# First product stage of a hybrid attention block: more buffers, and the output weights split one unit behind their load

## The chip, the cores and the metric

The kernel runs on one core of a Trainium2 chip. The metric is the device time of one execution in microseconds (us), the median over the runs of a kernel. TensorE is called PE and its weight loads PEld; VectorE is DVE, ScalarE is ACT, GpSimd is POOL, and SyncE is SP, which here issues nearly all of the DMAs. PEclk is the TensorE clock that was granted, as a share of full speed.

## The reference, cut to what matters

One layer of a streaming encoder on 2064 tokens (2048 and 16 learned ones) of width 1024. One projection W_in of 3592 columns feeds three groups of heads: a gated linear recurrence (RG-LRU), a forgetting attention and an RWKV-7 recurrence. Their outputs are joined and projected by W_out; a gated feed-forward part follows.

```python
h += rms_norm(W_out @ concat(rg_lru(p_a), forgetting_attention(p_b), rwkv7(p_c)), g_post)   # p = W_in @ rms_norm(h, g_pre)
h += rms_norm(W_down @ (gelu(g) * v), g_ffn_post)                  # [g | v] = causal_dwconv3(W_up @ rms_norm(h))
```

All is float32. The kernel keeps that precision by writing each factor as a high and a low part, hi = round(x) and lo = x - hi, and by adding three products: hi·hi, lo·hi and hi·lo (`mm3`, lines 172 to 174).

## The kernel before, in words

The program is written in a tile language. It names tiles from pools of so many buffers, and when the program is built, a scheduler with its own timing model fixes the order of the instructions on every engine, and which buffer each tile gets. On the chip each engine runs its list in that order. A tile that takes a buffer waits for the last reader of the tile that had it before, and an instruction that waits holds up all that stand behind it on its engine. `issue_after(ins)` puts the instructions of a block behind `ins` in the list of their engine.

**The first product stage** (to about 890 us) computes the projection in three parts of tokens, each of two blocks (400 and 384, 384 and 384, 256 and 256 tokens). `w_in_norm` normalises and transposes a part's rows: `norm_transpose` loads 128 rows to `xt`, an ACT Square to `xj` (L118) sums their squares, DVE scales `xt` (L130), PE transposes to `pst` (L143), and ACT and DVE write the parts `xh` and `xl` (L149, L150). `w_in_part` then does the gate columns (`fraw`, `fw`) and 24 units of 128 columns: 8 for RWKV-7 (c), 4 for the gated recurrence (a), 4 each for keys (k), values (v) and queries (q). A unit is 24 matmuls for each block into a PSUM tile `psp`. Part 0 loads raw weights and splits them into `wh` and `wl` (ACT L166, DVE L167), storing both in `scr_wk`; parts 1 and 2 load the pair from there (L216). Results of c and a leave as `stp` (L56 or L58, ACT and DVE in turns); those of k and q as `sth` and `stl` (ACT L234, DVE L235), each followed by its store; values are transposed and leave as `stv`.

**Beside the units** run the recurrences: `Beside` takes two steps of them per unit from unit 14 of a part on. They are `gate_block`, `Rwkv.block` (tiles whose names begin with `rw`, small products in `rps`, `eps`) and `lru_block` (tiles `rwlu`, `rwla`, `rwlr`; L1401 loads, L1408 is its first ACT step, and its result is stored to `scr_mix` from the buffer `lu`). They have buffers of their own. Two more jobs lie beside parts 1 and 2: `up_sums` on POOL, a step at every even unit, and `w_out_split`, a step at every odd unit of part 1: a load of 128 rows of W_out to `raw`, the ACT rounding (L166) and the DVE difference (L167) to two tiles `wo`, and two stores.

Pools: `nt` has four buffers of 4 KB a partition (tag `nt_x`: `xt`, raw weights, the three tiles of a W_out step), `w` has two each of `wh` and `wl`, and `st` two, but `stl` and `stv` one. After the stage come the attention (to about 1560 us), W_out and the feed-forward part.

Of the kernel before, what the change touches and what calls it, by code (L numbers as in the profile page):

```python
# [8 lines left out]
F32 = mybir.dt.float32  # L9
# [9 lines left out]
P = 128  # L19
D = 1024  # L20
# [12 lines left out]
class Core:  # L33


    def __init__(self, tc, ctx):
        self.tc = tc
        self.nc = tc.nc
        self.ctx = ctx
        self.uid = 0  # L40
        nc = self.nc
        self.const = ctx.enter_context(tc.tile_pool(name="const", bufs=1))
        self.ident = self.const.tile([P, P], F32, name="ident")
        make_identity(nc, self.ident[:])
        self.flip = 0
        self.root = self.apart = False

    def n(self, s):
# [3 lines left out]
    def evac(self, out, src):  # L52

        self.flip ^= 1
        if self.flip:
            self.nc.scalar.activation(out, src, AF.Copy)  # L56
        else:
            self.nc.vector.tensor_copy(out, src)  # L58
# [62 lines left out]

def norm_transpose(core, pools, psum, src, rows, gain, pieces):

    nc = core.nc
    xt = pools["nt"].tile([P, D], F32, tag="nt_x", name=core.n("xt"))
    nc.sync.dma_start(xt[:rows], src)
    junk = pools["st"].tile([P, D], BF16, tag="stv", name=core.n("xj"), bufs=1)
    v = pools["nt"].tile([P, 6], F32, tag="rs", name=core.n("rs"))
    rs = rstd_of(core, v[:rows], xt[:rows], D, junk[:rows])
    nc.vector.scalar_tensor_tensor(xt[:rows], xt[:rows], rs, gain[:rows], op0=ALU.mult, op1=ALU.mult)  # L130
    transpose_split(core, psum, xt, rows, pieces)
# [29 lines left out]
def load_parts(core, raws, src, hi, lo):  # L161

    pool, tag, bufs = raws
    raw = pool.tile(list(hi.shape), F32, tag=tag, name=core.n("raw"), bufs=bufs)
    core.loaded = core.nc.sync.dma_start(raw[:], src)
    core.nc.scalar.activation(hi, raw[:], AF.Copy)  # L166
    core.nc.vector.tensor_tensor(lo, raw[:], hi, op=ALU.subtract)  # L167
# [19 lines left out]
def w_in_norm(core, pools, psum, x, meta, gain, part):  # L187
    blocks = []
    for b, tl in enumerate(w_in_tokens(part)):
        t0 = tl[0][0]  # L190
        n = sum(r for _, r in tl)
        hi = pools["xn"].tile([P, KD, n], F32R, tag=f"xh{b}", name=core.n("xh"))
        lo = pools["xn"].tile([P, KD, n], F32R, tag=f"xl{b}", name=core.n("xl"))
        blocks.append((t0, n, tl, hi, lo))
    for t0, n, tl, hi, lo in blocks:
        for s, rows in tl:
            src = meta if s < META else x[s - META : s - META + rows, :]
            norm_transpose(core, pools, psum, src, rows, gain, [(hi, lo, s - t0, 0, rows)])
    return blocks
# [7 lines left out]
def w_in_weights(core, pools, w_in, c0, scr, part):  # L207

    if part == 0:
        src = w_in[:, c0 : c0 + P].rearrange("(k p) c -> p k c", p=P)  # L210
        pair = split_load(core, pools["w"], (pools["nt"], "nt_x", None), src, [P, KD, P], "w")
    else:
        pair = [pools["w"].tile([P, KD, P], F32R, tag=s, name=core.n(s)) for s in ("wh", "wl")]
    for t, kept in zip(pair, w_in_kept(scr, c0)):
        t = t[:].rearrange("p k c -> p (k c)").bitcast(F32)
        core.loaded = core.nc.sync.dma_start(*((kept, t) if part == 0 else (t, kept)))  # L216
    return pair


def w_in_step(core, pools, psum, weights, block, kind, c0, scr):  # L220
# [8 lines left out]
    if kind in ("q", "k"):  # L229
        sc = 0.125 if kind == "q" else 1.0  # L230
        r0 = c0 - (512 if kind == "q" else 1024)
        oh = st.tile([P, 400], F32R, tag="sth", name=core.n("sth"))
        ol = st.tile([P, 400], F32R, tag="stl", name=core.n("stl"), bufs=1)
        nc.scalar.activation(oh[:, :n], ps[:, :n], AF.Copy, scale=sc)  # L234
        nc.vector.scalar_tensor_tensor(ol[:, :n], ps[:, :n], sc, oh[:, :n], op0=ALU.mult, op1=ALU.subtract)  # L235
        nc.sync.dma_start(scr[kind + "h"][r0 : r0 + P, t0 : t0 + n], oh[:, :n].bitcast(F32))
        nc.sync.dma_start(scr[kind + "l"][r0 : r0 + P, t0 : t0 + n], ol[:, :n].bitcast(F32))
        return
# [7 lines left out]
    def turn():  # L246
# [3 lines left out]
        for i, (s, rows) in enumerate(tl):  # L250
            nc.tensor.transpose(pt[:rows, i], o[:, s - t0 : s - t0 + rows], core.ident[:])
        ot = st.tile([P, 4, P], F32, tag="stv", name=core.n("stv"), bufs=1)
        i0 = 0
# [15 lines left out]
def w_in_gate(core, pools, psum, w_in, blocks, scr, part):  # L269
# [5 lines left out]
    if part == 0:  # L275
        raw = pools["w"].tile([P, KD, 8], F32, tag="fraw", name=core.n("fraw"), bufs=1)
        nc.sync.dma_start(raw[:], w_in[:, c0 : c0 + 8].rearrange("(k p) c -> p k c", p=P))
# [6 lines left out]
    for t0, n, tl, hi, lo in blocks:  # L284
# [5 lines left out]
        nc.scalar.activation(a[:, :n], ps[32:40, :n], AF.Copy)  # L290
        o = pools["st"].tile([8, 400], F32, tag="stl", name=core.n("fo"), bufs=1)
        nc.vector.tensor_tensor(o[:, :n], ps[0:8, :n], a[:, :n], op=ALU.add)
# [585 lines left out]
def rwkv_consts(core, pool, psum, w):  # L878
# [70 lines left out]

    k["st"] = c.tile([P, 2, 64], F32, name="rstate")  # L950
    nc.vector.memset(k["st"][:], 0.0)


    u1 = c.tile([P, 256], F32, name="unit1")
    nc.vector.memset(u1[:], 0.0)
    nc.vector.memset(u1[:, 0:256:17], 1.0)
    u2 = c.tile([P, 128], F32, name="unit2")
    nc.vector.memset(u2[:], 0.0)
    nc.vector.memset(u2[0:64, 0:128:17], 1.0)
    nc.vector.memset(u2[64:128, 8:128:17], 1.0)  # L960
    k["unit"] = {1: u1, 2: u2}
    return k


class Rwkv:
# [127 lines left out]
    def chunks(self, b, nch, sg, rav, bk, wc, bon):  # L1093
# [54 lines left out]
        x3 = ix[:np_, : 16 * jw].rearrange("p (j s) -> p j s", s=16)  # L1148
        nc.vector.tensor_copy(ix[:np_, : 16 * jw], k["unit"][parts][:np_, :])
        nc.vector.memset(ia[:np_, 0:256:17], 1.0)  # L1150
# [96 lines left out]

        st = self.t([P, nch + 1, 2, 64], "st")
        nc.vector.tensor_copy(st[:, 0], k["st"][:])
        gain = self.ps().rearrange("p (c a t) -> p c a t", a=2, t=64)  # L1250
# [8 lines left out]
        for c in range(nch):  # L1259
# [7 lines left out]
            nc.vector.tensor_copy(st[:, c + 1], gain[:, c])  # L1267
        nc.vector.tensor_copy(k["st"][:], st[:, nch])
        yield
# [117 lines left out]
def lru_block(core, R, scr, k, b):  # L1387
# [8 lines left out]
    def tl(s):  # L1396
        return R.t([P, 256], s)[:, :n]

# [67 lines left out]
def w_out_split(core, pool, w_out, scr):  # L1466

    for k in range(KD):
        hi, lo = (pool.tile([P, D], F32R, tag="nt_x", name=core.n("wo")) for _ in range(2))
        load_parts(core, (pool, "nt_x", None), w_out[k * P : (k + 1) * P, :], hi[:], lo[:])  # L1470
        for i, t in enumerate((hi, lo)):
            core.nc.sync.dma_start(scr["wo"][k, i], t[:].bitcast(F32))
        yield
# [585 lines left out]
def hybrid_block_kernel(ctx: ExitStack, tc: tile.TileContext, args, out):  # L2059
# [25 lines left out]
    with ExitStack() as p1:  # L2085
# [7 lines left out]
        with ExitStack() as p1a:  # L2093
# [6 lines left out]
            for part in range(3):  # L2100
# [29 lines left out]
                for i, _ in enumerate(units, READY + 1 if part == 0 else 1):  # L2130
                    if i == READY + 1:
                        beside.add(recurrences(core, R, lk, a["fox_f_bias"], scr, blocks, part))
                    beside.advance()
                    if part and (i % 2 == 0 or part == 1 and i > 1):
                        with tc.issue_after(core.loaded.ins):
                            next(split_out if i % 2 else sums, None)
                run(sums) if part == 2 else None
# [182 lines left out]
```

## Time and profile before

| | before |
|---|---|
| median of 3 runs | 3050.18 us (3047.77 to 3064.09) |
| the profiled execution, its time | 3044.26 us |
| its span in the trace | 3042.5 us |
| granted PE clock over the span | 0.977 |
| busy: PE, PEld, DVE, ACT, POOL | 95%, 82%, 67%, 49%, 43% |
| DMA, mean over the span | 174 GB/s |

A busy share is the time in which an engine worked, over the span. Matmuls are pipelined, so a busy PE need not be PE at its peak: the weight loads run under the matmuls, and at a lower granted clock the same matmul is counted as busy for longer. In the views of the trace, a row of waits names the engine and its instruction, what released it, and the total, the number and the longest of those waits.

### The profile page before, as it was taken

How to read it: one execution, taken by the hardware profiler on the slowest of the kernel's cores; microseconds unless marked ns; L12 is line 12 of the kernel's file. 1: busy time of each engine (PE TensorE's matmuls, PEld its weight loads, DVE VectorE, ACT ScalarE, POOL GpSimd, SP SyncE). 2: the span in 40 equal slices, each digit the busy share in tenths (PEclk: the TensorE clock that was granted, in tenths of full speed). 3: DMA queues.
4: the chain of work that ended last, by engine and by line, in shares of the span. 5: the costliest groups of instructions: out<-in, count | busy, mean ns of one | idle time of the engine just before them, and what ended most of it. 6: DMA issues, size and time to landing. Idle time of an engine off the chain costs nothing. (4 is left out here: it accounts for less than half of the span.)

```text
span 3042.5 us, 52754 instructions
## 1 busy us (share of the span) xinstructions
PE 2901.8 (95%) x18694; PEld 2486.7 (82%) x18694; DVE 2043.7 (67%) x3947; ACT 1480.9 (49%) x2858; POOL 1309.2 (43%) x1567
## 2 busy tenths in 40 slices
PE   6998999999989998999989899999999999999998
PEld 6998898888876654565568899999999999787887
DVE  5268645656677885555736888888778777646666
ACT  4245342434346654454634656666666665434333
POOL 1001121122224656566843457545655544556443
PEclk9998999999998999999999999999999999999999
DMA  6776478565654347434326555567677764536453
GB/s 211 245 233 214 155 237 294 159 212 193 213 160 95 97 102 214 110 94 123 82 81 221 166 168 181 180 187 221 210 220 208 216 204 130 167 109 213 146 182 120
DMA packets 469189, 530.48 MB, mean 174 GB/s; under 512 B 85710, under 2 KB 355736, under 8 KB 467372
## 3 DMA queue, kind: packets, MB, share of 16 engines
q1 hardware_dynamic: 468156, 526.17, 56.6%
q8 instruction: 147, 2.41, 0.3%
q0 software_dynamic: 768, 0.93, 0.1%
q14 instruction: 118, 0.97, 0.1%
HBM read 368.07 MB, written 158.90 MB: 173 GB/s over the span
## 5 line engine op out<-in xcount | busy, mean ns | idle before, releaser
L172 PE MATMUL psu<-xo,uw 128*128 128x344 f32 x1848 | 591.3, 324 | 15.6 <-DVE vb L1812 7.9
L173 PE MATMUL psu<-xo,uw 128*128 128x344 f32 x1848 | 593.9, 322 | 0.0
L174 PE MATMUL psu<-xo,uw 128*128 128x344 f32 x1848 | 585.0, 321 | 0.7 <-DVE uw L1621 0.7
L172 PE MATMUL psp<-xh,wh 128*128 128x384 f32 (+2 forms) x1152 | 382.9, 332 | 4.2 <-ACT wh L166 3.1
L174 PE MATMUL psp<-xh,wl 128*128 128x384 f32 (+2 forms) x1152 | 380.3, 331 | 2.0 <-DMA wl<-scr_wk 1.8
L173 PE MATMUL psp<-xl,wh 128*128 128x384 f32 (+2 forms) x1152 | 379.5, 330 | 0.0
L172 PEld LDWEIGHTS psu<-xo,uw 128*128 128x128 f32 x1848 | 348.1, 189 | 19.1 <-DVE vb L1812 9.9
L1621 DVE TENSOR_TENSOR uw<-uq,uw 128x512 fp32r<-128x512 f32 x341 | 316.9, 936 | 67.9 <-ACT uw L1620 65.8
L173 PEld LDWEIGHTS psu<-xo,uw 128*128 128x128 f32 x1848 | 349.2, 189 | 0.0
L174 PEld LDWEIGHTS psu<-xo,uw 128*128 128x128 f32 x1848 | 347.7, 189 | 1.3 <-DVE uw L1621 1.2
L1620 ACT ACTIVATE uw<-uq 128x512 fp32r<-128x512 f32 x462 | 287.0, 627 | 105.0 <-PE psu L174 47.8
L686 ACT ACTIVATE p<-sc,bias 128x512 f32<-128x512 f32 (+4 forms) x352 | 197.4, 590 | 191.3 <-PE sc L682 159.1
L559 DVE TENSOR_REDUCE mc<-mx 128x1 f32<-128x512 f32 (+6 forms) x352 | 190.3, 564 | 105.2 <-PE mx L554 79.9
L1760 DVE SCALAR_TENSOR_TENSOR uy<-psu,ffn_cols,uy 128x342 f32<-128x342 f32 (+1 forms) x390 | 220.2, 566 | 57.4 <-ACT uy L1758 55.7
L1768 POOL TENSOR_TENSOR uy<-uy,uy 128x342 f32<-128x342 f32 (+1 forms) x132 | 139.3, 1056 | 249.8 <-DVE uy L1760 63.7
L1621 POOL TENSOR_TENSOR uw<-uq,uw 128x512 fp32r<-128x512 f32 x121 | 180.9, 1495 | 148.4 <-ACT uw L1620 130.5
L725 POOL TENSOR_TENSOR acc<-acc,p 128x512 f32<-128x512 f32 (+3 forms) x208 | 221.2, 1066 | 52.3 <-DVE acc L725 26.3
L174 PEld LDWEIGHTS psp<-xh,wl 128*128 128x128 f32 x1152 | 221.3, 192 | 11.5 <-issue 6.0
L172 PEld LDWEIGHTS psp<-xh,wh 128*128 128x128 f32 x1152 | 221.4, 192 | 11.0 <-issue 4.0
L173 PEld LDWEIGHTS psp<-xl,wh 128*128 128x128 f32 x1152 | 221.2, 192 | 7.7 <-issue 5.6
L1621 DVE TENSOR_TENSOR fo<-u,fo 128x896 fp32r<-128x896 f32 x88 | 100.1, 1138 | 132.7 <-ACT fo L1620 132.2
L1620 ACT ACTIVATE fo<-u 128x896 fp32r<-128x896 f32 x88 | 81.2, 923 | 207.1 <-PE psd L174 115.6
(483 smaller groups left out, 6399.2 us busy)
## 6 DMA issues: line engine op xcount, KB each, us to landing
uq<-scr_us SPq DMA_DIRECT2D x220, 256.0 KB
uq<-in_ffn_up_dram SPq DMA_DIRECT2D x209, 256.0 KB
wl<-scr_wk SPq DMA_DIRECT2D x48, 512.0 KB
wh<-scr_wk SPq DMA_DIRECT2D x48, 512.0 KB
u<-scr_ff SPq DMA_DIRECT2D x88, 256.0 KB
scr_ff<-uy SPq DMA_DIRECT2D x110, 171.0 KB
raw<-in_w_in_dram SPq DMA_DIRECT2D x24, 512.0 KB
scr_wk<-wh SPq DMA_DIRECT2D x24, 512.0 KB
```

What stands on the lines that cost most here:

```text
L172: nc.tensor.matmul(out, ah, bh, start=first, stop=False, skip_group_check=more)
L173: nc.tensor.matmul(out, ah, bl, start=False, stop=False, skip_group_check=more)
L174: nc.tensor.matmul(out, al, bh, start=False, stop=last, skip_group_check=more)
L559: self.reduced = nc.vector.tensor_reduce(mc[:rows, i, ci : ci + 1], ps[:rows, : e - a], axis=AX.X, op=ALU.max)
L686: last = nc.scalar.activation(p[:rows, :w], ps[:rows, :w], AF.Exp, bias=bias[:rows, j : j + 1])
L725: eng.tensor_tensor(a, ps_[0][0][:rows, c0:n] if start and i == 1 else a, p[:rows, : n - c0], op=ALU.add)
L1620: core.nc.scalar.activation(hi, src, AF.Copy)
L1621: (eng or core.nc.vector).tensor_tensor(lo, src, hi, op=ALU.subtract)
L1760: core.conved = stt(y[:, :n], src[:, i : n + i], cw[:, 44 * i + cc : 44 * i + cc + 1], y[:, :n], op0=ALU.mult, op1=ALU.add)
L1768: core.pooled = nc.gpsimd.tensor_tensor(v[:, :n], g[:, :n], v[:, :n], op=ALU.mult)
```

## The change

It has seven parts, all in the first product stage and the recurrences beside it.

1. `stl` (low parts of keys and queries, and the gate's result `fo`) and the tag `stv` (values, the junk output `xj` of the Square, and now the raw gate columns `fraw`) get two buffers instead of one.
2. The tile `lu` of `lru_block` gets two buffers instead of one.
3. In part 2, two of every four units take their weight pair from `nt_x` instead of the pool `w`.
4. `w_out_split` loads its raw rows one step ahead and yields; the next step rounds them on ACT behind the latest PSUM copy there (`core.acted`), and the loads and stores stand behind the latest weight load on SP. It takes 16 steps, at every unit of part 1 but the first, instead of 8 at the odd ones.
5. The Squares of part 1's rows, but for the first two tiles, stand behind the last weight rounding of part 0 on ACT (`core.rounded`).
6. `fraw` moves from the pool `w` to `stv`.
7. The RWKV state becomes one lasting tile of five chunk states, written in place, so that one copy per block of 256 tokens goes; a constant (`unit1`) becomes two memsets where it is used.

```diff
@@ norm_transpose
-    junk = pools["st"].tile([P, D], BF16, tag="stv", name=core.n("xj"), bufs=1)
+    junk = pools["st"].tile([P, D], BF16, tag="stv", name=core.n("xj"))
     v = pools["nt"].tile([P, 6], F32, tag="rs", name=core.n("rs"))
-    rs = rstd_of(core, v[:rows], xt[:rows], D, junk[:rows])
+    with after():
+        rs = rstd_of(core, v[:rows], xt[:rows], D, junk[:rows])
@@ load_parts
-    core.nc.scalar.activation(hi, raw[:], AF.Copy)
+    core.rounded = core.nc.scalar.activation(hi, raw[:], AF.Copy)
@@ w_in_norm
+            late = part == 1 and (s, rows) not in blocks[0][2][:2]
+            after = (lambda: core.tc.issue_after(core.rounded.ins)) if late else nullcontext
@@ w_in_weights
-        pair = [pools["w"].tile([P, KD, P], F32R, tag=s, name=core.n(s)) for s in ("wh", "wl")]
+        core.turns += part == 2
+        pl, tags = (pools["nt"], ("nt_x", "nt_x")) if core.turns % 4 > 1 else (pools["w"], ("wh", "wl"))
+        pair = [pl.tile([P, KD, P], F32R, tag=tag, name=core.n(s)) for s, tag in zip(("wh", "wl"), tags)]
@@ w_in_step
-        ol = st.tile([P, 400], F32R, tag="stl", name=core.n("stl"), bufs=1)
-        nc.scalar.activation(oh[:, :n], ps[:, :n], AF.Copy, scale=sc)
+        ol = st.tile([P, 400], F32R, tag="stl", name=core.n("stl"))
+        core.acted = nc.scalar.activation(oh[:, :n], ps[:, :n], AF.Copy, scale=sc)
...
-        ot = st.tile([P, 4, P], F32, tag="stv", name=core.n("stv"), bufs=1)
+        ot = st.tile([P, 4, P], F32, tag="stv", name=core.n("stv"))
@@ w_in_gate
-        raw = pools["w"].tile([P, KD, 8], F32, tag="fraw", name=core.n("fraw"), bufs=1)
+        raw = pools["st"].tile([P, KD, 8], F32, tag="stv", name=core.n("fraw"))
...
-        o = pools["st"].tile([8, 400], F32, tag="stl", name=core.n("fo"), bufs=1)
+        o = pools["st"].tile([8, 400], F32, tag="stl", name=core.n("fo"))
@@ Rwkv.block
-        st = self.t([P, nch + 1, 2, 64], "st")
-        nc.vector.tensor_copy(st[:, 0], k["st"][:])
+        st = k["st"]
+        nc.vector.tensor_copy(st[:, 0], st[:, 4])
...
-        nc.vector.tensor_copy(k["st"][:], st[:, nch])
@@ lru_block
-        return R.t([P, 256], s)[:, :n]
+        return R.t([P, 256], s, bufs=2 if s == "lu" else 1)[:, :n]
@@ w_out_split
+        raw = pool.tile([P, D], F32, tag="nt_x", name=core.n("raw"))
+        with core.tc.issue_after(core.loaded.ins):
+            core.nc.sync.dma_start(raw[:], w_out[k * P : (k + 1) * P, :])
+        yield
         hi, lo = (pool.tile([P, D], F32R, tag="nt_x", name=core.n("wo")) for _ in range(2))
-        load_parts(core, (pool, "nt_x", None), w_out[k * P : (k + 1) * P, :], hi[:], lo[:])
-        for i, t in enumerate((hi, lo)):
-            core.nc.sync.dma_start(scr["wo"][k, i], t[:].bitcast(F32))
+        with core.tc.issue_after(core.acted.ins):
+            core.nc.scalar.activation(hi[:], raw[:], AF.Copy)
+        core.nc.vector.tensor_tensor(lo[:], raw[:], hi[:], op=ALU.subtract)
+        with core.tc.issue_after(core.loaded.ins):
+            for i, t in enumerate((hi, lo)):
+                core.nc.sync.dma_start(scr["wo"][k, i], t[:].bitcast(F32))
         yield
@@ hybrid_block_kernel
-                    if part and (i % 2 == 0 or part == 1 and i > 1):
+                    if part == 1 and i > 1:
+                        next(split_out, None)
+                    if part and i % 2 == 0:
                         with tc.issue_after(core.loaded.ins):
-                            next(split_out if i % 2 else sums, None)
+                            next(sums, None)
```

The scheduler then deals the order anew. PE's instructions are as many as before, the first that stands elsewhere is the 985th of 16342, and from the feed-forward part on the order is that of before; between them, in the attention too, it differs in many places. Three places matter below.

The first is ACT at the end of part 0, where the roundings of the last raw weights (`wh`) meet the Squares (`xj`) of part 1's rows. Before:

```order
L118 ACTIVATE xj_3113,rs_3114<-xt_3111 128x1024
L166 ACTIVATE wh_2863<-raw_2865 128x1024
L234 ACTIVATE sth_2583<-psp_2558 128x384
L1063 ACTIVATE rwsq_2101<-rwe_2089,rwkv_om 128x256 x2
L234 ACTIVATE sth_2707<-psp_2682 128x400
L118 ACTIVATE xj_3142,rs_3143<-xt_3140 128x1024
L166 ACTIVATE wh_2871<-raw_2873 128x1024
L234 ACTIVATE sth_2738<-psp_2713 128x384
```

The same place after:

```order
L119 ACTIVATE xj_3108,rs_3109<-xt_3106 128x1024
L168 ACTIVATE wh_2858<-raw_2860 128x1024
L240 ACTIVATE sth_2580<-psp_2555 128x384
L240 ACTIVATE sth_2704<-psp_2679 128x400
L168 ACTIVATE wh_2866<-raw_2868 128x1024
L119 ACTIVATE xj_3137,rs_3138<-xt_3135 128x1024
L240 ACTIVATE sth_2735<-psp_2710 128x384
```

The last rounding of part 0 (`wh_2871`, now `wh_2866`) stood behind the fourth tile's Square, and stands ahead of it now.

The second is SP in part 1, where rows of W_out are loaded (`raw` from `in_w_out_dram`) and their split is stored (`scr_wo`). Before, around one step:

```order
L216 DMA wh_4858<-scr_wk 128x1024
L216 DMA wl_4859<-scr_wk 128x1024
L243 DMA scr_p<-stp_4717 128x384
L165 DMA raw_5017<-in_w_out_dram 128x1024
L236 DMA scr_kh<-sth_4757 128x384
L237 DMA scr_kl<-stl_4758 128x384
L1472 DMA scr_wo<-wo_5015 128x1024
L1472 DMA scr_wo<-wo_5016 128x1024
```

After, around the store of one step and the load of the next:

```order
L249 DMA scr_p<-stp_4684 128x384
L1484 DMA scr_wo<-wo_4715 128x1024
L1476 DMA raw_4841<-in_w_out_dram 128x1024
L1406 DMA rwlraw_6018<-scr_p 128x256
L1484 DMA scr_wo<-wo_4716 128x1024
L222 DMA wh_4853<-scr_wk 128x1024
L222 DMA wl_4854<-scr_wk 128x1024
```

A load stood three rows ahead of the store of its own split; now it stands between the two stores of the step before it, and its own rounding comes a unit later.

The third is SP at the beginning of part 2, with the loads of the weight pairs from `scr_wk`. Before:

```order
L283 DMA fw_6693<-scr_wk 128x1024
L216 DMA wl_6853<-scr_wk 128x1024
L236 DMA scr_qh<-sth_6411 128x384
L237 DMA scr_ql<-stl_6412 128x384
L1645 DMA us_6984<-in_ffn_up_dram 128x2x128 x4
L216 DMA wh_6852<-scr_wk 128x1024
L216 DMA wl_6995<-scr_wk 128x1024
```

After:

```order
L289 DMA fw_6684<-scr_wk 128x1024
L222 DMA wl_6842<-scr_wk 128x1024
L242 DMA scr_qh<-sth_6402 128x384
L1657 DMA us_6973<-in_ffn_up_dram 128x2x128 x2
L243 DMA scr_ql<-stl_6403 128x384
L1657 DMA us_6973<-in_ffn_up_dram 128x2x128 x2
L998 DMA rwraw_7251<-scr_p 128x2x257
L222 DMA wh_6841<-scr_wk 128x1024
L222 DMA wl_7190<-scr_wk 128x1024
L222 DMA wh_6983<-scr_wk 128x1024
```

The load of `wl_7190`, of the fourth unit, now stands ahead of the pair of the second.

More of the change, by code (lines that the diff above doesn't have):

```diff
@@ L46, in __init__ @@
         self.root = self.apart = False
+        self.turns = 0
     def n(self, s):
@@ L55, in evac @@
         if self.flip:
-            self.nc.scalar.activation(out, src, AF.Copy)
+            self.acted = self.nc.scalar.activation(out, src, AF.Copy)
         else:
@@ L119, in rstd_of, with norm_transpose @@
     return rstd_from(core.nc, v, ss, width, core.apart)
-def norm_transpose(core, pools, psum, src, rows, gain, pieces):
+def norm_transpose(core, pools, psum, src, rows, gain, pieces, after=nullcontext):
     nc = core.nc
@@ L197, in w_in_norm @@
             src = meta if s < META else x[s - META : s - META + rows, :]
-            norm_transpose(core, pools, psum, src, rows, gain, [(hi, lo, s - t0, 0, rows)])
+            late = part == 1 and (s, rows) not in blocks[0][2][:2]
+            after = (lambda: core.tc.issue_after(core.rounded.ins)) if late else nullcontext
+            norm_transpose(core, pools, psum, src, rows, gain, [(hi, lo, s - t0, 0, rows)], after)
     return blocks
@@ L948, in rwkv_consts @@
     k["rst"] = rst
[L950 to L956, printed above, removed]
+    k["st"] = c.tile([P, 5, 2, 64], F32, name="rstate")
+    nc.vector.memset(k["st"][:, 4], 0.0)
     u2 = c.tile([P, 128], F32, name="unit2")
@@ L960, in rwkv_consts @@
     nc.vector.memset(u2[64:128, 8:128:17], 1.0)
-    k["unit"] = {1: u1, 2: u2}
+    k["unit"] = u2
     return k
@@ L1148, in chunks @@
         x3 = ix[:np_, : 16 * jw].rearrange("p (j s) -> p j s", s=16)
-        nc.vector.tensor_copy(ix[:np_, : 16 * jw], k["unit"][parts][:np_, :])
+        if parts == 2:
+            nc.vector.tensor_copy(ix[:np_, : 16 * jw], k["unit"][:np_, :])
+        else:
+            nc.vector.memset(ix[:np_], 0.0)
+            nc.vector.memset(ix[:np_, 0:256:17], 1.0)
         nc.vector.memset(ia[:np_, 0:256:17], 1.0)
```

## The prediction

> **What bounds the kernel now.** I read the page first, for which engine is the bound, then the table by stretches, for where that engine is not full.
>
> ```profile
> span 3042.5 us, 52754 instructions
> PE 2901.8 (95%) x18694; PEld 2486.7 (82%) x18694; DVE 2043.7 (67%) x3947; ACT 1480.9 (49%) x2858; POOL 1309.2 (43%) x1567
> ```
>
> PE works for 95% of the span, so a change that removes no product can give back only what PE idles and what it loses at a lower clock. The change lies before 890 us. The table has a stretch to a row: its length, the busy time of PE, PEld, DVE, ACT and POOL, then PEclk, DMA share and GB/s. The last row is the attention.
>
> ```profile
> 0.00:42.00 42.00, 18.78 (x79) 16.16 (x80) 32.50 (x157) 17.55 (x33) 10.56 (x30) 1.00 0.69 211
> 42.00:250.00 208.00, 207.94 (x1174) 199.93 (x1173) 90.20 (x176) 82.76 (x143) 9.68 (x19) 1.00 0.70 227
> 250.00:300.00 50.00, 41.89 (x287) 38.21 (x286) 42.31 (x117) 25.73 (x51) 3.84 (x5) 0.83 0.71 242
> 300.00:600.00 300.00, 292.21 (x2467) 264.35 (x2467) 170.44 (x419) 113.80 (x214) 58.67 (x96) 0.98 0.64 211
> 600.00:890.00 290.00, 281.78 (x2911) 254.49 (x2906) 182.12 (x464) 117.56 (x241) 61.06 (x101) 0.98 0.60 194
> 1010.00:1560.00 550.00, 515.95 (x2829) 309.18 (x2828) 341.63 (x739) 287.09 (x547) 363.86 (x488) 0.97 0.44 111
> ```
>
> From 42 to 250 us PE is full: nothing is to be had. In the three rows from 250 to 890 it idles 8.1, 7.8 and 8.2 us, 24 together. Next I asked PE's waits from 42 to 890 us, for what those are.
>
> ```profile
> PE rps L1179 <- DVE rwxu L1195: 3.1, 2, 2.0
> PE psp L172 <- ACT wh L166: 3.1, 1, 3.1
> PE rps L1141 <- DVE rwbk L1135: 2.6, 1, 2.6
> PE pst L143 <- DVE xl L150: 2.5, 2, 2.0
> PE eps L1415 <- DVE rwlu L1410: 1.9, 2, 1.1
> PE psp L174 <- DMA wl<-scr_wk: 1.8, 2, 1.3
> PE eps L1037 <- ACT ncref L436: 1.7, 1, 1.7
> PE rps L1320 <- ACT rww L1327: 1.3, 1, 1.3
> PE psp L172 <- DMA wh<-scr_wk: 1.1, 1, 1.1
> PE eps L1067 <- DVE rwix L78: 0.9, 1, 0.9
> PE rps L1179 <- ACT rwsc L1142: 0.8, 1, 0.8
> PE rps L1179 <- DVE rwxu L1189: 0.8, 1, 0.8
> PE pst L143 <- DVE xt L130: 0.5, 1, 0.5
> ```
>
> Many short waits, no long one. Beside them stands the clock. The same table over the places where it was low, each a few us long:
>
> ```profile
> 262.00:267.00 5.00, 5.00 (x21) 5.00 (x21) 4.89 (x14) 0.42 (x2) 0.00 (x0) 0.66 0.92 297
> 286.00:300.00 14.00, 10.03 (x100) 8.82 (x101) 13.81 (x40) 12.13 (x23) 0.87 (x1) 0.53 0.65 231
> 348.00:352.00 4.00, 4.00 (x15) 3.75 (x13) 1.87 (x5) 0.00 (x0) 0.00 (x0) 0.57 0.84 320
> 409.00:413.00 4.00, 3.91 (x12) 3.68 (x13) 2.25 (x8) 1.26 (x3) 2.16 (x6) 0.58 0.96 274
> 501.00:509.00 8.00, 7.49 (x23) 6.67 (x24) 3.33 (x5) 3.00 (x7) 0.92 (x1) 0.57 1.00 362
> 675.00:683.00 8.00, 7.27 (x58) 7.15 (x58) 5.76 (x14) 2.63 (x7) 1.93 (x4) 0.57 0.28 91
> 686.00:690.00 4.00, 4.00 (x22) 3.27 (x22) 2.15 (x6) 3.95 (x8) 0.16 (x1) 0.57 0.49 156
> 774.00:778.00 4.00, 4.00 (x36) 3.96 (x33) 3.49 (x10) 2.10 (x4) 2.67 (x3) 0.61 0.12 42
> ```
>
> Length times (1 - PEclk) is the work lost: 1.7, 6.6, 1.7, 1.7, 3.4, 3.4, 1.7 and 1.6 us, together 21.8. So the stage can give back at most 24 + 22 = 46 us, 1.5% of the kernel, and only what hangs on the buffers, loads and orders that the change touches. To find that I followed the waits one engine back, to ACT:
>
> ```profile
> ACT wo L166 <- DMA raw<-in_w_out_dram: 28.9, 6, 11.6
> ACT rwlu L1408 <- DMA scr_mix<-rwlu: 19.6, 8, 4.7
> ```
>
> and to the instructions ahead of the waits on their engines (start, duration, then in brackets the idle time before and its releaser):
>
> ```profile
> 259.56 1.06 ACT L118 ACTIVATE xj<-xt 128x1024 bf16<-128x1024 f32 x1 [6.77 <-DMA xt<-in_x_dram]
> 260.61 1.04 ACT L166 ACTIVATE wh<-raw 128x1024 fp32r<-128x1024 f32 x1
> 283.69 0.56 DVE L235 SCALAR_TENSOR_TENSOR stl<-psp,sth 128x384 fp32r<-128x384 f32 x1 [2.27 <-DMA scr_ql<-stl]
> 482.38 1.06 ACT L166 ACTIVATE wo<-raw 128x1024 fp32r<-128x1024 f32 x1 [6.83 <-DMA raw<-in_w_out_dram]
> 567.22 1.19 PE L1179 MATMUL rps<-rwxu,rwsc 32*32 32x32 f32 x32 [2.00 <-DVE rwxu L1195]
> 670.54 0.60 ACT L1408 ACTIVATE rwlu<-rwlraw,lru_cols 128x256 f32<-128x256 f32 x1 [4.48 <-DMA scr_mix<-rwlu]
> ```
>
> **The change part by part.**
>
> *Squares behind the rounding (part 5).* At 259.56 us a Square of the next part's rows waits 6.77 us for its load on ACT, and the rounding that PE needs stands right behind it. That is PE's 3.1 us (`psp` for `wh`), and the low clock at 262 us follows. With the rounding ahead, only its 1.04 us remains before the product, and the raw rows are there. Gain 3.1 + 1.7 = 4.8 us. What is late next is the Square, which the next part's transposes need some 25 us later.
>
> *Two buffers for `stl` and `stv` (part 1), and the boundary of parts 0 and 1.* At 283.69 us DVE waits 2.27 us for the store of the tile before; a second buffer ends that. The stretch 286 to 300 us is where the next part's rows are transposed and the recurrence starts. PE waits there for DVE's `xl` (2.0 of the 2.5), `rwbk` (2.6) and `xt` (0.5), 5.1 us, and loses 6.6 at the low clock: 11.7 in all. But DVE is busy for 13.81 of those 14 us. What the change takes off it there is waits before the stretch, and a W_out step beside it; the work itself stays. The ends are 0 (DVE is the bound whatever precedes) and 11.7 (all was lateness brought along). I take half, 5.9 us.
>
> *Two buffers for `lu` (part 2).* `rwlu` on ACT waits 8 times, 19.6 us, for the store of the block before, and the gated recurrence's products wait behind: `eps` for `rwlu` 1.9, and, since ACT is late then (the row of 670.54 us), `rps` for `rwsc` 0.8 and one `rwxu` of 1.1 (the 3.1 less the 2.0 at 567 us). The low clock at 409 and at 675 us comes right behind such waits, 1.7 and 3.4. Gain 1.9 + 0.8 + 1.1 + 1.7 + 3.4 = 8.9 us. The buffer has no other user, so nothing is paid.
>
> *W_out split a unit behind its load (part 4).* Roundings on ACT wait 28.9 us in 6 waits for rows loaded just before, mostly with nothing urgent behind them. At 482.38 us there is: 6.83 us, and `rww`, for which PE then waits 1.3. With the load a unit ahead that wait goes: 1.3 us. The work is the same, eight roundings, eight differences and 24 transfers. On SP a load now stands ahead of the next unit's weight pair and needs a free one of the four `nt_x` buffers. Three are taken by the step in work, the fourth is free once the stores of the step before have landed, a unit earlier; I charge nothing. If they had not, the pair behind would come late as it does in part 2 now, 1.1 or 1.3 us a time.
>
> *Four pairs in flight in part 2 (part 3).* PE's waits for `wl` and `wh` from `scr_wk`, 1.8 + 1.1 us, lie in part 2, where a unit takes two thirds of the time and its pair is loaded just ahead of its use. With twice the pairs they go: 2.9 us, no low clock with them.
>
> *State in place and the constant (part 7).* One DVE copy less and one memset more per block, beside full PE: nothing, either way.
>
> *Start (part 6, and the order there).* Before 42 us DVE is the busiest, 32.5 of 42 us, and PE waits for it. `fraw` is loaded later, behind others, and one weight difference moves ahead of a row scaling on DVE; against that some constants move behind. A weight difference takes
>
> ```profile
> L167 DVE TENSOR_TENSOR wl<-raw,wh x1: 1212/1212/1212, 29.6 to 29.6; 128x1024 fp32r<-128x1024 f32 x1
> ```
>
> 1.2 us. One such step on the path, and its load awaited for as long again, cost 3 us at worst; the constants out of the way gain 1. I take a loss of 1 us.
>
> *The order dealt anew.* Not all recurrence waits have a cause that the change names: `ncref` 1.7, `rwxu` 2.0 and 0.8, `rwix` 0.9, with the low clock at 348 and 501 us (1.7 and 3.4), 10.5 us. In a new order such waits fall elsewhere, and where one wait is removed the next latest shows. I charge half as much again, 5.3 us (0 to 10.5).
>
> The sum: 4.8 + 5.9 + 8.9 + 1.3 + 2.9 = 23.8 gained, 1.0 + 5.3 = 6.3 lost, net 17.5 us. On the profiled execution, 3044.26 us (1.8 above its span), that gives 3026.8; it ran 5.9 us under the median of the runs, 3050.18, and from that the forecast is 3033 us.
>
> **Waits and the clock.** More than half of what I count at the first boundary and at `lu` is low clock that I put down to waits. The rows bear that out in part: low clock follows the waits of 3.1 us at 259 and those near 670, but none was shown behind the 2.0 us at 567, and at 686 and 774 us the clock fell with PE at 4.00 of 4.00 us busy, with no wait at all.
>
> [...]
>
> **The rivals.**
>
> *Only the waits go.* The low clock comes from stretches of small products (686 and 774 us speak for it; 262 and 675 us against) and stays. Then the gain is 3.1 + 2.55 (half the boundary's 5.1) + 3.8 + 1.3 + 2.9 = 13.7, less 1.0 and the wait half of the new order's price, 2.7: 10 us, 3040. With the boundary unmoved it is 7.5, 3043. Chance 0.33.
>
> *The boundary falls whole.* DVE comes to 286 us without its backlog, the 11.7 us go and nothing steps in: 23.8 + 5.9 - 1 = 28.7 us, 3021. For it: DVE stood waiting before the stretch, in which it is the bound; against: 13.81 of 14 us of work stay. Chance 0.17.
>
> *Slower: the attention's new order.* The instructions there are the same, dealt anew, and PE waits in this stage for ACT's exponentials:
>
> ```profile
> PE sc L681 <- ACT p L686: 9.5, 18, 2.0
> ```
>
> The stage idles 550 - 515.95 = 34 us and loses 0.03 x 550 = 16.5 at the lower clock, 50.5 together. If exponentials or their neighbours come behind other work more often and idle time and low clock grow by two thirds, 34 us are lost, and 17.5 are gained: 3066. It decides once the growth is over 17.5 + 15 = 33 us. Against it: POOL at 66% and DVE at 62% there have slack, and the data are ready long before. Chance 0.11.
>
> *The change does nothing that counts.* The new order puts waits of the same size in the same places, and the gains and the 10.5 us of new waits, with 3 at the start, cancel: about 3050. Chance 0.08; my own forecast keeps 0.31.
>
> **How the numbers follow.** A difference of 0.5%, 15 us, is about what a measurement of this kernel can tell from none: below 3035 is faster, above 3065 slower. The forecast's case lies on the faster side with 0.31 of which 0.06 ends just over the bound by the unknown half of the boundary; the whole boundary adds 0.17, and of the waits-only case, whose windows may partly go, 0.09 end below 3035: faster 0.51. Slower is the attention's case, by its point of decision 0.07 above 3065, and 0.03 from several costs at once: 0.10. The rest, 0.39, is the same. The range goes down past the whole boundary (3021) by the start's gain of 1, the 0.2% between the profiled execution and the median (5.9) and 2 for waits not listed, to 3012, and up to the do-nothing case, 3050, with 2 over it, 3052. Outside lie the attention's case and a tenth of the rest.
>
> **What would show it.** In the trace of the changed kernel: no wait of `psp` for ACT's `wh`, and PEclk near 1 around 262 us; no waits of `rwlu` for the store to `scr_mix`, and full clock around 409 and 675 us; no waits of `wo` for `in_w_out_dram`, none of `psp` for `scr_wk` in part 2; the stretch that answers to 286 to 300 us shorter by about 6 us; the end of the stage some 17 us earlier, and the attention as long as before. I am wrong if the clock stays low where the waits went, if DVE fills the boundary as before, or if the attention is longer by more than 10 us.

## The result, and the profile after

The changed kernel took 3035.84 us (median of 10 runs, 3032.95 to 3043.01), the kernel before 3048.60 us (10 runs, 3042.67 to 3064.09): a ratio of 0.9957, 95% interval 0.9943 to 0.9970. A second measurement, with 8 runs of the change beside 25 of before, gave 3038.12 and 3055.14 us, 0.9946 (0.9927 to 0.9965). So the gain is 13 to 17 us, near the 0.5% that the prediction took as the least that a measurement of this kernel can tell; the forecast was 17.5 us, from 3050.18 to 3033 us.

The two profiled executions hide it. That of before, 3044.26 us, is one of the fastest of its kernel, and that of the change, 3043.01, is the slowest of its ten; their spans in the trace, 3042.5 and 3041.3 us, differ by 1.2 us. A second profile of each is among the experiments, with spans of 3054.7 and 3037.8 us.

The first lines of the page of the changed kernel:

```profile
span 3041.3 us, 52749 instructions
PE 2907.9 (96%) x18694; PEld 2494.9 (82%) x18694; DVE 2024.5 (67%) x3937; ACT 1481.0 (49%) x2858; POOL 1314.3 (43%) x1567
```

The table by stretches of the changed kernel, with the columns of before:

```profile
250.00:300.00 50.00, 43.44 (x411) 38.63 (x410) 44.56 (x124) 27.24 (x53) 8.59 (x15) 0.91 0.72 239
300.00:600.00 300.00, 295.98 (x2393) 268.60 (x2393) 168.06 (x409) 109.12 (x206) 55.87 (x85) 0.96 0.66 219
600.00:890.00 290.00, 278.75 (x2851) 253.61 (x2849) 178.81 (x457) 118.63 (x241) 62.91 (x100) 0.95 0.59 187
1010.00:1560.00 550.00, 515.13 (x2825) 310.12 (x2823) 330.31 (x730) 285.68 (x542) 365.71 (x495) 0.97 0.44 112
```

In the stretch from 300 to 600 us PE idles 4 us where it idled 8; from 600 to 890 it idles 11 where it idled 8. The clock is lower in both, 0.96 and 0.95 for 0.98. PE's waits from 42 to 890 us:

```profile
PE rps L1185 <- DVE rwxu L1201: 6.3, 4, 2.9
PE eps L1039 <- ACT rwe L1041: 4.9, 1, 4.9
PE pst L145 <- DVE xl L152: 3.3, 2, 1.8
PE rps L1185 <- ACT rwsc L1144: 2.4, 2, 1.8
PE rps L1185 <- DMA xt<-in_x_dram: 2.0, 1, 2.0
```

Most of the waits that the prediction named are gone: `psp` for ACT's `wh`, `eps` for `rwlu`, `rps` for `rww`, `psp` for `wl` and `wh` from `scr_wk`, also `ncref`. Three are not: `pst` for `xl` is 3.3 us (2.5 before), `rps` for `rwsc` 2.4 (0.8) and `rps` for `rwxu` (now L1201) 6.3 (3.1). Beside them stand others of the recurrences, the longest now 4.9 us where it was 3.1. The low clock is gone at 262, at 348 and at 501 us, and is longer elsewhere (the same table over such places):

```profile
260.00:266.00 6.00, 6.00 (x32) 5.52 (x32) 5.89 (x15) 1.86 (x3) 0.00 (x0) 1.00 0.85 292
291.00:314.70 23.70, 23.54 (x229) 20.19 (x227) 19.48 (x55) 14.17 (x28) 7.35 (x11) 0.50 0.19 65
344.00:352.00 8.00, 8.00 (x97) 7.23 (x96) 5.66 (x11) 1.96 (x4) 4.09 (x4) 1.00 0.84 277
407.00:413.60 6.60, 5.64 (x43) 5.22 (x44) 3.91 (x8) 0.91 (x3) 0.00 (x0) 0.50 0.43 132
500.00:509.00 9.00, 9.00 (x47) 7.98 (x47) 4.08 (x7) 5.16 (x11) 0.62 (x1) 1.00 1.04 403
670.00:680.00 10.00, 5.62 (x28) 4.57 (x29) 9.28 (x21) 5.64 (x12) 4.49 (x8) 0.50 0.27 87
```

What stands on ACT ahead of the 4.9 us:

```profile
667.92 0.60 ACT L1413 ACTIVATE rwlu<-rwlraw,lru_cols 128x256 f32<-128x256 f32 x1 [0.82 <-DMA scr_mix<-rwlu]
668.43 0.49 ACT L1431 ACTIVATE rwlr<-rwlr,lru_rate 128x256 f32<-128x256 f32 x1
668.94 1.28 ACT L1436 ACT_TABLE_LOAD   x1
671.75 0.42 ACT L1436 ACTIVATE rwlr<-rwlr 128x256 f32<-128x256 f32 x1 [1.53 <-DVE rwlr L1435]
672.19 1.28 ACT L1041 ACT_TABLE_LOAD   x1
673.48 0.84 ACT L1041 ACTIVATE rwe<-eps,rwkv_om 128x256 f32<-128x256 f32 x2
```

The gated recurrence waits less for its store here (0.82 us, 4.48 before), and `rwe`, for which the next RWKV product waits, stands in this order behind its square root (L1436), behind what that waits for on DVE, and behind two table loads of 1.28 us. The second `lu` has not ended the waits for the store, as ACT's waits from 42 to 890 us show:

```profile
ACT rwlu L1413 <- DMA rwlraw<-scr_p: 23.8, 7, 5.5
ACT rwlu L1413 <- DMA scr_mix<-rwlu: 8.3, 5, 3.6
```

Those for the store are 8.3 us in 5 waits where they were 19.6 in 8. Those for the load of the next input, `rwlraw`, are 23.8 in 7 where they were 7.9 in 2, so that the first instruction of the gated recurrence waits for its transfers some 32 us in all, where it waited 27.5.

### The profile page after: what moved, and what is told of

The parts are those of the page before. It is cut to its first block, busy times and chain, and to the rows that moved or that the text cites. A ratio compares the mean times of both kernels' runs of the same rounds, so it can differ in the third digit from the quotient of the medians.

```text
span 3041.3 us, 52749 instructions
## 1 busy us (share of the span) xinstructions
PE 2907.9 (96%) x18694; PEld 2494.9 (82%) x18694; DVE 2024.5 (67%) x3937; ACT 1481.0 (49%) x2858; POOL 1314.3 (43%) x1567
## 4 chain that ended last, share of the span: by engine, by line
PE 41%; DVE 3%; DMA 2%; POOL 2%; issue 2%; ACT 1%; DVEq 0%; SPq 0%; POOLq 0%; ACTq 0%
PE psu L174 8%; PE psu L175 8%; PE psu L176 8%; PE psd L174 4%; PE psd L175 4%; PE psd L176 4%; PE pswo L174 1%; PE pswo L176 1%; PE pswo L175 1%; DMA xt<-scr_h 1%; DVE uw L1633 1%; DVE uy L1772 1%; POOL dw L1633 0%; PE pst L1599 0%; DVE xo L1633 0%
## 5 line engine op out<-in xcount | busy, mean ns | idle before, releaser
L565 DVE TENSOR_REDUCE mc<-mx 128x1 f32<-128x512 f32 (+5 forms) x352 | 190.3, 566 | 113.5 <-PE mx L560 90.1
```

Source lines behind the costliest of these rows:

```text
L565: self.reduced = nc.vector.tensor_reduce(mc[:rows, i, ci : ci + 1], ps[:rows, : e - a], axis=AX.X, op=ALU.max)
```

## The experiments

Each was timed beside the kernel before; the ratios are to it, with their 95% intervals. The kernels are the one before with single parts of the change, or the changed kernel without single parts. The scheduler deals the order anew for each, so none differs by its edit alone, and that turned out to be the main thing to measure.

**Both kernels profiled once more.** Edit: none.

> The kernel before, unchanged, profiled once more. Theory 1 (the low clock hangs on the waits of the program): the same waits of PE between 42 and 890 us (about 24 us), and the low clock at the same eight places, about 22 us lost. [...]

> The changed kernel, unchanged, profiled once more. [...] Theory 1: the waits and the low clock of the first profile again, 31 us lost from 42 to 890 us and 0.80 granted over the first 42 us. [...]

Measured: the kernel before at 1.0005 (0.9993 to 1.0018), the changed one at 0.9946 (0.9927 to 0.9965). The waits came again, as PE's waits from 42 to 890 us in the second profile of before show:

```profile
PE psp L172 <- ACT wh L166: 3.2, 1, 3.2
PE pst L143 <- DVE xl L150: 2.6, 2, 2.1
PE rps L1141 <- DVE rwbk L1135: 2.6, 1, 2.6
```

Of the eight places of low clock six came again. Two did not, those at 409 and 686 us, and three are new, at 567, 731 and 868 us. The table over these five, in the second execution:

```profile
409.00:413.00 4.00, 3.56 (x19) 3.45 (x20) 2.39 (x8) 1.61 (x4) 2.39 (x5) 1.00 0.97 286
567.60:571.00 3.40, 3.40 (x13) 3.40 (x12) 1.97 (x4) 0.98 (x2) 0.00 (x0) 0.50 0.80 255
686.00:692.00 6.00, 6.00 (x59) 5.17 (x58) 2.15 (x6) 5.93 (x10) 0.62 (x1) 1.00 0.46 146
731.40:734.80 3.40, 3.06 (x15) 2.77 (x14) 0.99 (x5) 2.22 (x4) 0.00 (x0) 0.50 1.06 404
867.90:874.70 6.80, 6.80 (x54) 6.30 (x53) 5.34 (x12) 2.78 (x7) 1.41 (x3) 0.50 0.37 126
```

The first execution at two of the new places:

```profile
563.40:574.00 10.60, 8.60 (x112) 7.88 (x107) 7.44 (x16) 2.26 (x4) 1.81 (x3) 1.00 0.64 210
727.90:735.70 7.80, 6.11 (x49) 5.70 (x48) 3.54 (x16) 3.88 (x6) 0.00 (x0) 1.00 1.01 349
```

It passed the waits at 567 and 731 us at full clock, and in the second the low clock comes right behind them. The waits were not the same to the tenth: at 409, 567 and 731 us the execution whose clock fell was the one with the longer wait (1.14 for 0.63 us, 2.28 for 2.00, 1.79 for 1.13).

In the second profile of the change the waits came again too (4.5 us for `rwe`, 2.9 for `rwxu`), and five of its seven places of low clock, at 291, 407, 625, 670 and 769 us. Summed as in the prediction, over steps of 4 us from 42 to 890 us, the low clock takes 31 us in both profiles of the change, 22 and 24 in those of before. So theory 1 does not hold as it stands: most places belong to the program, some to the one execution, and of a low clock seen once only the part that comes again can be put down to the program.

**The buffers alone.** Edit on the kernel before, with `fraw` and the state moved as in the change, to make room for them (two of its lines, others are left out):

```diff
-    junk = pools["st"].tile([P, D], BF16, tag="stv", name=core.n("xj"), bufs=1)
+    junk = pools["st"].tile([P, D], BF16, tag="stv", name=core.n("xj"))
...
-        return R.t([P, 256], s)[:, :n]
+        return R.t([P, 256], s, bufs=2 if s == "lu" else 1)[:, :n]
```

> The kernel before with two buffers for stl, stv and lu, and with fraw and the state moved as in the change, which makes the room for them; the weights of the last third, the split of W_out and the Squares stay as before. By my sum (boundary 5.9, lu 8.9, less 1 at the start and some 3 for the new order): 11 us faster, ratio 0.9965; waits of rwlu for the store to scr_mix gone. Rival (the gain comes from the other parts, the waits that these buffers end are followed by the next latest): within 3 us of before, ratio 0.999 to 1.001.

Measured: 0.9955 (0.9940 to 0.9971), 3041.81 us, as the sum said and as much as the whole change. That is no proof of its terms: in this profile, of an execution 4 us slower than the median, the first stage ends at 897 us, later than before, and the waits of `rwlu` for the store are 8.2 us and not gone. Where the gain lies it does not show.

**The old split of W_out in the changed kernel, and the new split alone in the kernel before.** The edit is part 4 of the change, taken back or put in.

> The changed kernel with the split of W_out as it was before: a step at every odd unit, load and rounding in one step. By my sum 1.3 us is lost again: ratio to before 0.9961 (the change had 0.9957), ACT waits some 25 us again for in_w_out_dram. Rival (the split behind its load is what clears ACT at the boundary and in part 1, and so most of the gain): ratio 0.998 to 1.000.

> The kernel before with the split of W_out alone as in the change (load a step ahead, rounding behind the latest PSUM copy, 16 steps). The changed kernel with the old split was 27 us faster than before, with the new one 15. Theory S (the new split itself costs, by its place on ACT at every unit): some 10 us slower than before, ratio 1.003. Theory L (any new order of the recurrences against the units moves the time by up to 10 us, and the split is only what dealt it anew): anything from 0.997 to 1.003, and where PE waits longer, it waits for a recurrence step behind other recurrence steps, not behind a rounding of W_out. My sum of the prediction: 1.3 us faster, 0.9996.

Measured: without the new split 0.9909 (0.9886 to 0.9932), 3028.28 us, faster than the change; with it alone 1.0063 (1.0041 to 1.0086), 3072.12 us. Both lie outside all that was expected. The new split loses both times, some 10 and 17 us, but not by one price at one place. In the second kernel the first stage ends where it did before, and the way from there to the last product of W_out takes 817.8 us where it took 785.1 (in an execution 6 us slower than the median). PE's waits from 900 to 1560 us, first of that kernel:

```profile
PE mx L554 <- DMA k<-scr_cl: 12.6, 5, 3.9
PE sc L681 <- ACT p L686: 11.7, 26, 2.2
```

and of before, beside the 9.5 us for `p` that the prediction shows:

```profile
PE mx L554 <- DMA k<-scr_cl: 5.0, 3, 2.4
```

These two are 10 us more. That is not the larger part of the 33, as the table shows over the whole stretch and over the end of the recurrences and the beginning of the attention, first of this kernel, then of before:

```profile
889.40:1707.20 817.80, 750.15 (x4295) 482.53 (x4296) 501.34 (x1112) 395.51 (x793) 451.54 (x611) 0.93 0.46 119
890.00:1010.00 120.00, 108.56 (x931) 77.29 (x928) 89.11 (x243) 56.76 (x126) 48.71 (x77) 0.74 0.48 107
```

```profile
890.10:1675.20 785.10, 726.34 (x4280) 470.28 (x4280) 505.58 (x1120) 395.48 (x792) 452.77 (x611) 0.96 0.47 124
890.00:1010.00 120.00, 100.86 (x953) 71.43 (x953) 97.90 (x274) 61.78 (x136) 50.89 (x82) 0.87 0.50 112
```

PE idles 9 us more over the stretch and is busy 24 us longer with the same products, at a lower clock. From 890 to 1010 us, where PE idles less than before, the clock is 0.74 for 0.87. So the slower rival of the prediction came in a kernel with one part of the change, in its outcome: the attention is late by idle time and low clock. The exponentials, on which the rival put it, have the smaller part (11.7 us of waits for 9.5), and much of the clock's loss lies ahead of the 1010 us from which it counted.

**Only the order swapped.** No operation differs; a unit's side jobs are written ahead of its recurrence steps. In the changed kernel (the edit shown), in the one with the old split, and in the kernel before:

```diff
-                    beside.advance()
                     if part == 1 and i > 1:
                         next(split_out, None)
                     if part and i % 2 == 0:
                         with tc.issue_after(core.loaded.ins):
                             next(sums, None)
+                    beside.advance()
```

> The changed kernel with nothing but the order in which a unit's side jobs are written swapped: the step of W_out's split and of the sums ahead of the two recurrence steps. No operation differs. Theory S: as the changed kernel, ratio to before 0.994 to 0.996. Theory L: 5 us or more away from it, 0.990 to 0.998 (a lesser difference speaks for S), by waits of rps and eps that stand at other places.

> The same swap on the changed kernel with the old split of W_out, which ran at 0.991 of before. Theory S: 0.990 to 0.992 again. Theory L: 0.993 to 0.998, that order having been a lucky one.

> The kernel before with nothing but the swap of the side jobs' order in a unit (W_out's split and the sums ahead of the recurrence steps). The same swap cost 0.4% in the changed kernel and 0.5% with the old split. If that is the swap's own price: ratio 1.004 to 1.005. If it is the order dealt: anywhere from 0.994 to 1.006, and where it is slower, the attention is longer while PE's idle time and low clock before the end of the first stage stay near 47 us.

Measured: 0.9987 (0.9971 to 1.0002), 0.9958 (0.9941 to 0.9976) and 0.9997 (0.9983 to 1.0011). The same swap costs 12 and 15 us in two kernels and nothing in the third, so it has no price of its own. The theory of the order (L) had this, though in the changed kernel the time lies above its range. There the swap takes back most of the gain, with the same operations on every engine: an order can be worth nearly as much as the whole change.

**The late Squares left out.** Edit: part 5 taken back.

> The changed kernel with the Squares of part 1's rows free to stand ahead of the last weight roundings, as before. By my sum 4.8 us are lost again: PE waits some 3 us for ACT's wh near 260 us and the low clock follows; ratio to before 0.996 to 0.997 where the change had 0.995. Rival (with two buffers for the junk output the Square no longer stands in the way): the change's time within 2 us.

Measured: 0.9908 (0.9881 to 0.9936), 3026.11 us, faster than the change by more than both theories allow. PE's one wait from 250 to 270 us, in that kernel:

```profile
PE psp L173 <- ACT wh L167: 0.4, 1, 0.4
```

So the wait of 3.1 us for which part 5 was made is already down to 0.4 with the other parts, at full clock from 258 to 272 us; part 5 is not needed here. The two other kernels with the buffers and without part 5 have 1.2 and 0.3 us there. Why part 5 costs 11 us no view shows; the swaps moved as much by the order alone. And this kernel, the fastest of all, has the wait for `rwe` at its longest:

```profile
PE eps L1036 <- ACT rwe L1038: 6.1, 1, 6.1
```

**One buffer for `lu` in the changed kernel.**

```diff
-        return R.t([P, 256], s, bufs=2 if s == "lu" else 1)[:, :n]
+        return R.t([P, 256], s)[:, :n]
```

> The changed kernel with one buffer for lu, as before. By my sum 8.9 us are lost again: ratio to before 0.998, ACT waits about 20 us for the store to scr_mix, and the products of the gated recurrence wait behind. Rival (with two buffers the gated recurrence ran into the RWKV steps and PE waited for those instead, 4.9 us for rwe at 674 and 2.9 for rwxu at 408 us): these two waits are gone, and the time is that of the change or up to 8 us under it, ratio 0.992 to 0.995.

Measured: 0.9957 (0.9943 to 0.9972), the changed kernel's time. ACT's waits for the store are 11.5 us, not the 20 expected. Its two stretches, from 42 us to the end of the first stage and from there to the last product of W_out, ahead of the same of the changed kernel's first profile:

```profile
42.00:870.40 828.40, 813.47 (x6800) 749.49 (x6799) 484.11 (x1174) 338.87 (x643) 133.37 (x218) 0.98 0.67 216
870.40:1672.90 802.50, 745.74 (x4303) 483.34 (x4304) 503.92 (x1110) 396.30 (x794) 450.28 (x612) 0.93 0.47 121
```

```profile
42.00:888.30 846.30, 824.47 (x6802) 759.26 (x6801) 485.21 (x1179) 339.53 (x645) 137.10 (x218) 0.96 0.65 212
888.30:1672.40 784.10, 732.52 (x4298) 477.12 (x4299) 489.33 (x1105) 396.18 (x791) 453.43 (x612) 0.94 0.47 124
```

PE's waits in the first stage of the kernel with one `lu`, for the two that the rival named:

```profile
PE eps L1039 <- ACT rwe L1041: 0.7, 1, 0.7
PE rps L1185 <- DVE rwxu L1201: 0.4, 1, 0.4
```

The 4.9 us for `rwe` are 0.7 and the 6.3 for `rwxu` are 0.4, as the rival had it; the first stage is 18 us shorter, with 15 us of idle PE in place of 22 and the clock at 0.98. And then the stretch behind it takes 18 us more, at 0.93, and the time is the same. That the second `lu` brings these waits is not shown by it: with two `lu` and the old split the wait of 4.9 us is gone as well (that for `rwxu` is 4.2), with two `lu` and the swap it is 5.8, and the swap alone ends the first stage 8 to 10 us earlier. The waits belong to the order that was dealt, of which the buffer can be one cause among others.

**Two weight pairs in part 2.** Edit: part 3 taken back.

> The changed kernel with two weight pairs in flight in part 2, as before. By my sum 2.9 us are lost again, in waits of psp for wh and wl from scr_wk after 700 us: ratio to before 0.996. Rival (the order decides, not the pairs): anywhere from 0.990 to 1.000, with the difference to the change outside part 2 as much as in it.

Measured: 0.9961 (0.9947 to 0.9975). From 700 to 890 us of that kernel:

```profile
PE psp L175 <- DMA wl<-scr_wk: 4.4, 4, 1.6
```

The waits came back, 4.4 us where none was in the change and 2.9 in the kernel before, and the time is that of the sum. With an interval of 4 us to either side that fits both theories; the waits alone are shown.

**The two omissions together.** Edit: parts 4 and 5 taken back.

> The change without the late Squares and with the old split of W_out: the buffers, the moved state, and the four pairs of part 2. Either omission alone gave 0.991. If the parts add up: 0.991 + 0.991 - 0.995 = 0.987, 40 us faster than before. If the order dealt decides: 0.990 to 0.998, no better than either alone.

Measured: 0.9976 (0.9966 to 0.9987), 3048.77 us. Each omission gave 0.991, both give less than the change itself. The parts do not add up.

All profiles side by side; the end of the first stage is that of the last `psp` product, and the second length goes to the end of the last W_out product. The kernel before is the measure, 1 (measured again 1.0005).

| kernel | ratio | first stage ends, us | from there to W_out's end, us |
|---|---|---|---|
| before, two profiles | 1 | 890.1, 895.2 | 785.1, 791.4 |
| before, swapped | 0.9997 | 894.1 | 786.1 |
| before with the new split | 1.0063 | 889.4 | 817.8 |
| before with the buffers | 0.9955 | 897.4 | 782.5 |
| change, two profiles | 0.9957, 0.9946 | 888.3, 886.1 | 784.1, 786.2 |
| change, swapped | 0.9987 | 878.1 | 798.7 |
| change, one `lu` | 0.9957 | 870.4 | 802.5 |
| change, two pairs | 0.9961 | 884.3 | 791.4 |
| change, old split | 0.9909 | 880.4 | 779.6 |
| change, old split, swapped | 0.9958 | 884.3 | 797.3 |
| change, no late Squares | 0.9908 | 881.0 | 780.1 |
| change, neither | 0.9976 | 897.3 | 786.1 |

The stage's end moves over 27 us and the stretch behind it over 38 us, with the same products in all. The two fastest, without the new split or without the late Squares, beat the kernel before and the changed one; a version with both omissions, which a sum would have chosen, does not.

## Why the prediction was right, and where its steps were not

The number was right: 3033 forecast, 3035.84 measured, a gain of 13 to 17 us for 17.5. But the sum reached it by errors that cancel, and in that it was luck. By the means of two profiles each, the first stage ends 5.5 us earlier (887.2 for 892.7), and the stretch behind it is 3.1 us shorter (785.2 for 788.3), of the 9.0 by which the mean spans differ (3039.6 for 3048.6); I had put all 17.5 in the first. The two profiles of before differ by as much as these parts, 5.1 and 6.3 us, so the division is rough.

*The rounding ahead of the Square, 4.8 us*: right in what was seen, the wait gone and the clock at 1.00 from 260 to 266 us. But the credit to part 5 is not borne out; without it the wait is 0.4 us.

*The boundary, 5.9 us of 0 to 11.7*: mis-sized, it is the lower end or under it. PE idles less there, 6.6 us for 8.1 from 250 to 300, but the clock is at half for 23.7 us from 291 where it was for 14 from 286. "DVE is the bound whatever precedes" was not the reason for this: DVE is busy for 19.48 of the 23.70 us and PE for 23.54, and PE's products there run at 0.50.

*`lu`, 8.9 us*: the wrong step. The sum took the waits for the store as ended. They are down from 19.6 to 8.3 us and not gone, and the waits for the load beside them are up by 16 us. Of the 8.9, 5.1 us were low clock at 409 and 675 us, and there it is at half for 6.6 and 10.0 us now. "The buffer has no other user, so nothing is paid" looked at the buffer and not at the engines: in the order that was dealt, the steps of the gated recurrence stand in the way of the RWKV steps on ACT, and PE's longest waits for the RWKV steps went from 2.6 us to 4.9 and 2.9. With one `lu` those two are gone and the time is the same, so the 8.9 us are not found in it.

*W_out's split, 1.3 us, and the pairs, 2.9 us*: the waits went, as named, and those for the pairs came back without part 3. For the split "I charge nothing" is not borne out: both kernels with it are slower than their partners, though not by late weight pairs (with the split alone PE waits 1.9 us for them, 2.9 before).

*Start, a loss of 1 us*: the sign was wrong. The products `psp`, of before and of the change, by the starts of the first and the last:

```profile
L172 PE MATMUL psp<-xh,wh x1152: 274/337/882, 42.1 to 888.4; 128*128 128x384 f32 x94, 128*128 128x256 f32 x64, 128*128 128x400 f32 x34
L174 PE MATMUL psp<-xh,wh x1152: 274/337/882, 40.8 to 887.8; 128*128 128x384 f32 x95, 128*128 128x256 f32 x64, 128*128 128x400 f32 x33
```

The first begins at 40.8 us, in the second profile at 40.1, where it began at 42.1 and 42.9; in all kernels with `fraw` moved it begins between 39.1 and 41.7 us, in those without between 42.1 and 43.1. PE has no pause from there to 250 us, so these 2 us are kept.

*The order dealt anew, 5.3 us of 0 to 10.5*: mis-sized the most. The swaps show 0 to 15 us for an order alone, and with the new split alone the stretch behind the stage came out 26 to 33 us longer. By these runs it is the largest term of all and can have either sign; an order that is dealt anew belongs in the range, not in the sum.

Of the rivals, "only the waits go" has the clock's part right in sum: it did not come back (0.97 to 0.96 over the first stage). Place by place it is not right, since at 348 and 501 us, behind waits of 0.9 and 1.7 us that are gone, the clock is full now. And not every low stretch is one of waits: the longest, 23.7 us from 291 us, has PE idle for 0.16 us. The slower rival did not come in the change and did come, in its outcome, with the new split alone.

What stays open is why one order of the stretch behind the stage takes 780 us and another 818. The rows name waits for `k`, `mc` and `p` and a clock of 0.92 to 0.96; low clock has the larger part in the one case that was taken apart. No run held the order still while one wait was changed, so the cause was not isolated. Nor was it shown which of the gain's 13 to 17 us is the buffers' own and which the order's: the kernels with two or more of the wider buffers lie between 0.9908 and 0.9987, those without between 0.9997 and 1.0063. That speaks for the buffers, but no view shows by which wait.

## What to carry to other kernels

When a scheduler orders the engines, a buffer that shortens a wait also lets other work move: ask what the freed steps will wait for next and which engine they will crowd, not only which wait goes. Measure a neutral change of order first, because its spread (here 15 us) is the least effect that a single edit can be credited with. And take two profiles of each kernel before a few us are put down to anything; one pair here showed 1.2 us of a gain of 13 to 17.

## What the runs showed of the hardware

The clock was at 0.50 in stretches of 3.40, 6.80 and 23.70 us in the rows above, and one program at the same place ran at a low clock in one execution and at full speed in the other: from 409 to 413 us at 0.58 in the first of the kernel before and at 1.00 in the second, from 567.6 to 571 us at 1.00 in the first and at 0.50 in the second. The longest such stretch of the first stage, 23.7 us in the changed kernel, had PE busy for 99% of it (23.54 us) at 0.50. These are its largest groups, with the number, the busy time and the mean ns of one:

```profile
L145 PE MATMUL pst<-ident,xt 128*128 128x128 f32 x16 | 4.2, 428 | 0.0
L1039 PE MATMUL eps<-rwwa,wa_up 64*128 64x256 f32 x8 | 4.1, 671 | 0.0
L1225 PE MATMUL rps<-rww,rwsc 64*64 64x64 f32 x32 | 3.9, 314 | 0.0
L293 PE MATMUL psf<-xh,fw 128*128 128x384 f32 x6 | 3.3, 546 | 0.0
```

Transposes and products of 64 rows and fewer make up most of it, beside 12 products of 128 rows for the gate columns (L293 and L294, 6.4 us together), and the clock stayed at 0.50 while PE was busy with these.
